# Preparing the next attention group inside the last head of the group ahead of it

## The chip, the cores and the metric

The kernel runs on one core of a Trainium2 chip. The metric is the device time of one execution in microseconds (us). The core has five engines with queues of their own: TensorE (PE in the rows, its weight loads PEld), VectorE (DVE), ScalarE (ACT), GpSimd (POOL) and SyncE (SP); POOL and SP also issue the DMAs.

## What is computed

Two transformer blocks on 512 tokens of width 1024, in float32. The second block runs two mixers on the same input, an RWKV-7 recurrence and a sparse attention (NSA) of 16 heads in 4 groups that share keys and values, merges them by gates, and goes on with a cross attention and a feed-forward part. The change lies in the sparse attention, which for each head sums three branches, each with a gate of its own:

```python
s_c = einsum(qb, k_cmp) * scale + group_bias(...)        # compressed keys: 31 of them
p_c = masked_softmax(s_c, ...)
o_c = einsum(p_c, v_cmp)
...
p_s = masked_softmax(s_s, (dist_s >= 0)...)              # selected blocks
o_s = einsum(p_s, v_g)
...
p_w = masked_softmax(s_w, m_w...)                        # window
o_w = einsum(p_w, vw_b)
out = gb[..., 0:1] * o_c + gb[..., 1:2] * o_s + gb[..., 2:3] * o_w
```

At 512 tokens the selection takes every block and the window covers the sequence, so branches 1 (selected) and 2 (window) are both causal attention over 512 keys, with different keys and values.

## The kernel before

The matmuls take float32 operands split into a high and a low part. `split` makes such a pair from one tile: ScalarE casts the high part (L162), VectorE subtracts it to get the low one (L163). For scores, `q_stack` (L285 on ScalarE, L286 on VectorE) puts both parts of a head's queries into one tile, and `k_stack` loads a key twice by two DMAs (`k_load`, L292) and splits it.

Tiles come from tagged pools with a fixed number of slots. The program is written as generators; a scheduler then sets the order of the instructions of each engine, with the order in which they are emitted as their priority. A tile's writer waits until the readers of the slot's last tile are done.

The phase "pa2" (L1452 on) weaves three streams by rates: `nsa` (190), the RWKV back part followed by the merge (240), and tiles of the merge gates (65). Each `yield` of a stream says how much it has emitted. RWKV's tiles carry the names psa_b and psb_b, the merge gates' psg_m. The loads of `nsa` go to POOL's queue (`self.side`), as do the merge gates' weights (ws).

`nsa` takes the groups g = 0 to 3 in pairs. A pair loads its values and splits them into the tile vt (L1117 to L1120; one slot). Then each group does its preparation and its four heads:

- preparation: four query stacks from two loads, the key stack of branch 1 from a third load, the key stack of branch 2 by a load that is issued here; a memset of kz on POOL (L1128) and copies of the compressed keys into it (L1130); eight matmuls for the compressed scores (L1134), the bias added (L1135), transposes (L1138), the softmax (L1142 to L1154, with the Exp on ScalarE at L1147), transposes back (L1157), and the split into the pair pc; then a `yield`
- for each head: the bias load (L1169, two slots), the product of pc and the compressed values into the PSUM bank pso (L1174), then for branches 1 and 2 the function `attend`, with a `yield` behind each. `attend` does the scores (L311, L312), the reduction with the bias (L313 on VectorE), the Exp (L315), the scaling (L321, L323), the transposes (L328), the split of the transposed probabilities into pt (L330, L331) and the products with vt (L332, L333). `o_evac` (L340, L341) then moves pso into the tile o, and after every second head o is stored to ynd (L1183) from SP's queue. The merge later reads ynd back (cast at L1202)

At head 2 of a group `nsa_loads` issues the loads for the next group: two of queries (L1051), the bias of the compressed scores (L1053, a tile of tag f) and the key of branch 1. All keys, queries and values share the three slots of the tag ld.

Other lines of the rows: L842 (a ScalarE copy of RWKV's), L834, L852, L858 and L883 (others of its copies), L777 and L778 (its solve on VectorE), L875, L889 and L897 (its state steps), L874 (its matmul), L957 (the evacuation of a merge-gate tile), L222 and L209 (the cast and the load of weights).

Of the kernel before, what the change touches and what calls it, by code (L numbers as in the profile page):

```python
# [38 lines left out]
class Gen:  # L39
# [998 lines left out]
    def nsa(self):  # L1038

        nc, A, V, S = self.nc, self.A, self.nc.vector, self.nc.scalar  # L1040
        self.ahead = self.nsa_loads(0)
        for gp in range(2):
            yield from self.nsa_groups(gp, *self.cmp)
# [67 lines left out]
    def nsa_groups(self, gp, kc, vc):  # L1111
        nc, A, V, S = self.nc, self.A, self.nc.vector, self.nc.scalar
        VT = self.f("vt", F32R, (128, 4 * 4 * 128)).rearrange("p (t k n) -> p t k n", t=4, k=4)
# [7 lines left out]
        for gl in range(2):  # L1121
            g = 2 * gp + gl
            qs, cb, k1 = self.ahead
            qst = {2 * i + par: self.q_stack(qs[i], par, -0.125) for i in range(2) for par in range(2)}
            kst = {1: self.split(k1, tag="kst"), 2: self.k_stack(self.kvd[6 + gp], gl)}

            kz = self.f("kz", F32R, (128, 448)).rearrange("p (i n) -> p i n", i=2)
            nc.gpsimd.memset(kz.bitcast(F32), 0.0)  # L1128
            for i, k in enumerate(kc):
                S.copy(kz[:, i, 96:128], k[:, 32 * g:32 * g + 32].bitcast(F32))  # L1130
            ps = self.ps("a")
            for h in range(4):
                for i in range(2):
                    nc.tensor.matmul(ps, kz[:, i, 96 - 32 * h:224 - 32 * h], qst[h], start=h + i == 0, stop=h + i == 4)  # L1134
            V.tensor_tensor(cb, ps, cb, OP.add)  # L1135
            ps = self.ps("b")
            for i in range(4):
                nc.tensor.transpose(ps[:, i * 128:i * 128 + 128], cb[:, i * 128:i * 128 + 128], self.ident)  # L1138
            v16 = ps.rearrange("p (a n) -> p a n", n=32)
            st = self.f("sm", shape=(128, 32))  # L1140
            m, s_ = st[:, 0:16], st[:, 16:32]
            V.tensor_reduce(m, v16, AX.X, OP.min)  # L1142
            V.tensor_scalar(m, m, 1e29, None, op0=OP.min)
            e = self.f("f")
            ev = e.rearrange("p (a n) -> p a n", n=32)
            V.tensor_tensor(ev, v16, m[:, :, None].to_broadcast([128, 16, 32]), OP.subtract)
            S.activation(e, e, AF.Exp, scale=-1.0)  # L1147
            V.tensor_reduce(s_, ev, AX.X, OP.add)
            V.tensor_scalar(s_, s_, 1e-30, None, op0=OP.max)
            V.reciprocal(s_, s_)  # L1150
            c0 = 12 * g
            V.tensor_tensor(s_.rearrange("p (i h) -> p i h", i=4), s_.rearrange("p (i h) -> p i h", i=4),
                            self.gt[:, :, c0:c0 + 12:3], OP.mult)
            V.tensor_tensor(ev, ev, s_[:, :, None].to_broadcast([128, 16, 32]), OP.mult)  # L1154
            ps = self.ps("b")
            for i in range(4):
                nc.tensor.transpose(ps[:, i * 128:i * 128 + 128], e[:, i * 128:i * 128 + 128], self.ident)  # L1157
            pc = self.split(ps, tag="pc")
            yield 6.0
            O = None  # L1160
            for h in range(4):
                hd = 4 * g + h
                par = h % 2
                if par == 0:
                    O = self.f("o")
                if h == 2 and g < 3:
                    self.ahead = self.nsa_loads(g + 1)
# [438 lines left out]
```

## Time and profile before

| | us |
|---|---|
| median of 3 runs | 2092.48 (2091.06 to 2099.59) |
| profiled execution | 2094.42, its span 2092.6 |
| mean granted TensorE clock | 0.975 of full |
| TensorE busy | 2015.6 (96%) |
| VectorE busy | 1308.9 (63%) |
| ScalarE busy | 926.1 (44%) |

The span is what the trace covers, from 0 to 2092.6 us; all times of rows are counted from its start. Busy shares are means over stages with different limits, so the stretches in the rows below are the view to go by. A row of a timeline gives the start, the duration of a run of like instructions, the engine, the line, the operation with output and inputs, and in brackets how long the engine idled before it and which instruction ended that.

### The profile page before, as it was taken

How to read it: one execution, taken by the hardware profiler on the slowest of the kernel's cores; microseconds unless marked ns; L12 is line 12 of the kernel's file. 1: busy time of each engine (PE TensorE's matmuls, PEld its weight loads, DVE VectorE, ACT ScalarE, POOL GpSimd, SP SyncE). 2: the span in 40 equal slices, each digit the busy share in tenths (PEclk: the TensorE clock that was granted, in tenths of full speed). 3: DMA queues.
4: the chain of work that ended last, by engine and by line, in shares of the span. 5: the costliest groups of instructions: out<-in, count | busy, mean ns of one | idle time of the engine just before them, and what ended most of it. 6: DMA issues, size and time to landing. Idle time of an engine off the chain costs nothing. (4 is left out here: it accounts for less than half of the span.)

```text
span 2092.6 us, 27828 instructions
## 1 busy us (share of the span) xinstructions
PE 2015.6 (96%) x9927; PEld 1635.5 (78%) x9927; DVE 1308.9 (63%) x3007; ACT 926.1 (44%) x1778; POOL 95.4 (5%) x167
## 2 busy tenths in 40 slices
PE   8999999999999999899989899999999999999999
PEld 7778888888887778777767688877878878888887
DVE  5785432554464569777668788878466756666522
ACT  5864531442253233233357477767143443333311
POOL 0000000000003201000120111000000000000000
PEclk9999999999999999999989799999999999999999
DMA  4223333333365655555574454445542123323332
GB/s 161 80 89 95 94 92 100 107 115 117 125 199 159 165 158 164 154 149 175 161 178 109 116 131 129 110 131 160 158 145 81 51 80 91 97 95 92 100 108 83
DMA packets 178266, 256.75 MB, mean 123 GB/s; under 512 B 95408, under 2 KB 109952, under 8 KB 178128
## 3 DMA queue, kind: packets, MB, share of 16 engines
q1 hardware_dynamic: 162832, 231.31, 38.1%
q0 software_dynamic: 15296, 23.66, 4.0%
q8 instruction: 79, 1.29, 0.3%
q14 instruction: 59, 0.48, 0.1%
HBM read 205.12 MB, written 45.53 MB: 120 GB/s over the span
## 5 line engine op out<-in xcount | busy, mean ns | idle before, releaser
L222 ACT CAST wh<-ws 128x1024 fp32r<-128x1024 f32 (+2 forms) x283 | 291.7, 1031 | 699.6 <-PE psg L244 459.4
L223 DVE TENSOR_TENSOR wl<-ws,wh 128x1024 fp32r<-128x1024 f32 (+2 forms) x283 | 339.5, 1201 | 263.5 <-ACT wh L222 262.3
L243 PE MATMUL psg<-xh,wh 128*128 128x512 f32 x984 | 392.1, 399 | 2.9 <-ACT wh L222 2.9
L245 PE MATMUL psg<-xh,wl 128*128 128x512 f32 x984 | 393.6, 400 | 0.0
L244 PE MATMUL psg<-act,wh 128*128 128x512 f32 x912 | 359.7, 395 | 1.1 <-DVE act L166 1.1
L243 PEld LDWEIGHTS psg<-xh,wh 128*128 128x128 f32 x984 | 185.9, 189 | 45.0 <-ACT wh L222 3.7
L245 PEld LDWEIGHTS psg<-xh,wl 128*128 128x128 f32 x984 | 186.1, 189 | 41.6 <-issue 1.2
L244 PEld LDWEIGHTS psg<-act,wh 128*128 128x128 f32 x912 | 171.1, 188 | 42.8 <-DVE act L166 1.5
L243 PE MATMUL psg<-act,wh 128*128 128x512 f32 x496 | 196.2, 397 | 2.8 <-ACT act L165 1.4
L245 PE MATMUL psg<-act,wl 128*128 128x512 f32 x496 | 196.0, 396 | 0.5 <-DVE wl L223 0.5
L244 PE MATMUL psg<-xl,wh 128*128 128x512 f32 x352 | 139.7, 397 | 0.0
L243 PEld LDWEIGHTS psg<-act,wh 128*128 128x128 f32 x496 | 92.8, 187 | 27.3 <-ACT act L165 2.2
L245 PEld LDWEIGHTS psg<-act,wl 128*128 128x128 f32 x496 | 93.0, 187 | 23.8 <-DVE wl L223 1.3
L315 ACT ACTIVATE p<-p,sm 128x128 f32<-128x128 f32 (+3 forms) x160 | 89.6, 561 | 18.8 <-DVE sm L313 17.7
L244 PE MATMUL psg<-x,wh 128*128 128x512 f32 x216 | 88.7, 411 | 0.0
L331 DVE TENSOR_TENSOR pt<-psb,pt 128x512 fp32r<-128x512 f32 (+3 forms) x160 | 75.6, 487 | 18.7 <-ACT pt L330 16.6
L313 DVE CUSTOM_DVE_ANT_0 p<-psa,bias 128x128 f32<-128x128 f32 (+3 forms) x160 | 76.0, 484 | 11.9 <-PE psa L312 9.7
L328 PE MATMUL psb<-ident,p 128*128 128x128 f32 x400 | 79.1, 292 | 2.2 <-DVE p L323 1.2
L330 ACT CAST pt<-psb 128x512 fp32r<-128x512 f32 (+3 forms) x160 | 65.9, 424 | 32.0 <-PE psb L328 29.4
L244 PEld LDWEIGHTS psg<-xl,wh 128*128 128x128 f32 x352 | 66.3, 188 | 14.1
L243 PE MATMUL psg_p<-xh,wh 128*128 128x512 f32 x176 | 72.8, 414 | 0.8 <-ACT f L957 0.6
L244 PE MATMUL psg_p<-x,wh 128*128 128x512 f32 x176 | 72.3, 411 | 0.0
(491 smaller groups left out, 3916.4 us busy)
## 6 DMA issues: line engine op xcount, KB each, us to landing
ws<-in_w_in SPq DMA_DIRECT2D x49, 512.0 KB, 4.0
ws<-in_w_fup SPq DMA_DIRECT2D x44, 512.0 KB, 3.5
ws<-in_w_up SPq DMA_DIRECT2D x32, 512.0 KB, 3.5
ws<-in_w_down SPq DMA_DIRECT2D x32, 512.0 KB, 3.6
ws<-in_w_fdn SPq DMA_DIRECT2D x16, 512.0 KB, 3.6
ws<-in_w_qku SPq DMA_DIRECT2D x12, 512.0 KB, 3.6
ws<-in_w_in POOLq DMA_DIRECT2D x10, 512.0 KB, 4.8
ws<-in_w_out SPq DMA_DIRECT2D x8, 512.0 KB, 3.5
```

The source lines that it names most:

```text
L222: nc.scalar.copy(wh[:, :n], ws[:, :n])
L223: nc.vector.tensor_tensor(wl[:, :n], ws[:, :n], wh[:, :n].bitcast(F32), OP.subtract)
L243: nc.tensor.matmul(p[:, :n], wh[:, s], h[:, :n], start=c + k == 0, stop=False)
L244: nc.tensor.matmul(p[:, :n], wh[:, s], l[:, :n], start=False, stop=False)
L245: nc.tensor.matmul(p[:, :n], wl[:, s], h[:, :n], start=False, stop=last)
L313: nc.vector.tensor_tensor_reduce(pt, ps[:, :w], bias[:, 512 - w:], 1.0, 3e38, OP.add, OP.min, m[:, i:i + 1])
L315: nc.scalar.activation(pt, pt, AF.Exp, bias=m[:, i:i + 1], scale=-1.0, accum_out=s[:, i:i + 1])
L328: nc.tensor.transpose(ps[:, (i - j) * 128:(i - j + 1) * 128], P[i][:, j * 128:j * 128 + 128], self.ident)
L330: nc.scalar.copy(ph[:, :w], ps[:, :w])
L331: nc.vector.tensor_tensor(pl[:, :w], ps[:, :w], ph[:, :w].bitcast(F32), OP.subtract)
```

## The change

`nsa_groups` is cut in three. `nsa_pre(g)` holds the query stacks, the key stack of branch 1, and the whole compressed softmax up to pc, with three yields of 2.0 in place of one of 6.0. `nsa_values(gp)` holds the values. `nsa_group(g, ...)` holds the key stack of branch 2, the values when g is even, and the heads. The preparation of group 0 is emitted at the start; that of group g + 1 is emitted in head 3 of group g, behind branch 1 and ahead of branch 2. The query stacks get five slots for four, the output tile o one for two. The loads for the next group stay at head 2.

```diff
@@ nsa
-        for gp in range(2):
-            yield from self.nsa_groups(gp, *self.cmp)
+        pre = yield from self.nsa_pre(0)
+        for g in range(4):
+            pre = yield from self.nsa_group(g, *pre)
@@ nsa_groups, nsa_pre, nsa_values
-    def nsa_groups(self, gp, kc, vc):
+    def nsa_pre(self, g):
...
+        qs, cb, k1 = self.ahead
+        qst = {2 * i + par: self.q_stack(qs[i], par, -0.125) for i in range(2) for par in range(2)}
+        kst = {1: self.split(k1, tag="kst")}
...
+        V.tensor_tensor(cb, ps, cb, OP.add)
+        yield 2.0
...
+        S.activation(e, e, AF.Exp, scale=-1.0)
+        yield 2.0
...
+        pc = self.split(ps, tag="pc")
+        yield 2.0
+        return qst, kst, pc
+
+    def nsa_values(self, gp):
...
-            kst = {1: self.split(k1, tag="kst"), 2: self.k_stack(self.kvd[6 + gp], gl)}
...
-            yield 6.0
@@ nsa_group
+    def nsa_group(self, g, qst, kst, pc):
...
+        kst[2] = self.k_stack(self.kvd[6 + gp], gl)
+        if gl == 0:
+            self.nsa_values(gp)
+        VT = self.VT
+        for h in range(4):
...
+            ready = self.nsa_pre(g + 1) if h == 3 and g < 3 else iter(())
+            for br in (1, 2):
+                kv = 2 * (br - 1) + gl
+                self.attend(qst[h], kst[br], bias, lambda j: VT[:, j, kv], o,
+                            False, br == 2, gate=self.gt[:, :, 3 * hd + br])
+                yield 3.6
+                if br == 1:
+                    try:
+                        while True:
+                            yield next(ready)
+                    except StopIteration as done:
+                        pre = done.value
+            self.o_evac(O, o, par)
...
@@ emit
-            with g.phase("pa2", f=3, ld=3, qst=4, kst=6, p=2, pt=4, bias=2, pc=2, kz=1, o=2, ot=1, vt=1,
+            with g.phase("pa2", f=3, ld=3, qst=5, kst=6, p=2, pt=4, bias=2, pc=2, kz=1, o=1, ot=1, vt=1,
```

The scheduled order shows where this puts the instructions. The numbers behind names tell tiles apart; they differ between the two programs.

ScalarE at the start of group 0, before (vt is the value tile, vs, wl, et and yi are RWKV's; kst_8959 is the key stack of branch 2):

```order
L162 CAST kst_8952<-ld_8926 128x512
L834 COPY wl_9004<-psa_b_9097 128x512
L1119 CAST vt_8929<-ld_8930 128x8x64
L842 COPY vs_9032<-psa_b_9103 64x4x64
L1119 CAST vt_8929<-ld_8935 128x8x64
L162 CAST kst_8959<-ld_8956 128x512
L1147 ACTIVATE f_8985<-f_8985 128x512
L842 COPY vs_9032<-psa_b_9103 64x4x64
L852 COPY et<-psa_b_9114 32x4x32 x4
```

The same place with the change (kst_9126 is the key stack of branch 2, f_9068 the Exp of the compressed softmax):

```order
L162 CAST kst_8941<-ld_8926 128x512
L834 COPY wl_8961<-psa_b_9054 128x512
L842 COPY vs_8989<-psa_b_9071 64x4x64
L162 CAST kst_9126<-ld_9123 128x512
L842 COPY vs_8989<-psa_b_9071 64x4x64
L1163 CAST vt_9130<-ld_9131 128x8x64
L1163 CAST vt_9130<-ld_9136 128x8x64
L852 COPY et<-psa_b_9082 32x4x32 x3
L1139 ACTIVATE f_9068<-f_9068 128x512
L852 COPY et<-psa_b_9082 32x4x32
```

The first copy into vs (L842) has moved ahead of the value casts, now L1163; the second stands behind the cast of branch 2's key stack, and the value casts and the Exp (now L1139) come last.

VectorE at the start of group 1, before (f_10344 and sm_10341 are the compressed softmax of group 1, bias_10441 is the bias of its head 0):

```order
L1152 TENSOR_TENSOR sm_10341<-sm_10341,gt 128x16
L897 SCALAR_TENSOR_TENSOR vs_9692<-vs_9692,decay,psb_b_10421 64x64
L1154 TENSOR_TENSOR f_10344<-f_10344,sm_10341 128x512
L777 TENSOR_TENSOR ys_9214<-as_9213,ys_9214 128x512
L897 SCALAR_TENSOR_TENSOR vs_9692<-vs_9692,decay,psb_b_10421 64x64
L778 TENSOR_REDUCE ys_9214<-ys_9214 128x16
L163 TENSOR_TENSOR pc_10358<-psb_10352,pc_10357 128x512
L313 ISA p_10447,sm_10446<-psa_10448,bias_10441 128x128
L313 ISA sm_10446 128x1
L313 ISA p_10447,sm_10446<-psa_10453,bias_10441 128x256
```

VectorE at the end of group 0 with the change (bias_9973 is the bias of group 0's head 3, pc_10305 the compressed probabilities of group 1; L154 and L155 are RWKV's norm):

```order
L153 TENSOR_TENSOR sm_10280<-sm_10277 128x8
L313 ISA p_10328,sm_10327<-psa_10334,bias_9973 128x256
L313 ISA sm_10327 128x1
L154 TENSOR_TENSOR sm_10280<-sm_10280,sm_10279 128x8
L313 ISA p_10328,sm_10327<-psa_10339,bias_9973 128x384
L313 ISA sm_10327 128x1
L155 SCALAR_TENSOR_TENSOR sm_10277<-sm_10280,sm_10277 128x8
L163 TENSOR_TENSOR pc_10305<-psb_10299,pc_10304 128x512
L313 ISA p_10328,sm_10327<-psa_10344,bias_9973 128x512
L313 ISA sm_10327 128x1
L777 TENSOR_TENSOR ys_9214<-as_9213,ys_9214 128x450
```

Before, group 1's softmax ended in the split into pc and its own head 0 followed; now that split stands among the score reductions of branch 2 of group 0's head 3, and the reductions of group 1's head 0 follow 19 rows behind this piece. The four reductions of that head's branch 1 stand 63 rows and more ahead.

POOL's queue at the same place, before (ld_10315 is the key load of branch 2 of group 1; ld_9745, ld_9747 and ld_9751 were the prefetch; bias_10441 and bias_10716 are for heads 0 and 1 of group 1):

```order
L292 DMA ld_9751<-kvd 64x512 x2
L1128 MEMSET kz_10322 128x448
L209 DMA ws_10644<-in_w_in 128x1024
L1169 DMA bias_9754<-grd 128x1x512
L1169 DMA bias_9973<-grd 128x1x512
L1169 DMA bias_10441<-grd 128x1x512
L1169 DMA bias_10716<-grd 128x1x512
L292 DMA ld_10315<-kvd 64x512 x2
L1051 DMA ld_10980<-qd 128x512
L1051 DMA ld_10982<-qd 128x512
```

The same queue with the change (ld_10433 is that key load, kz_10156 is for group 1's compressed scores):

```order
L1054 DMA f_9749<-gfd 128x1x512
L1119 MEMSET kz_10156 128x448
L1052 DMA ld_9745<-qd 128x512
L1052 DMA ld_9747<-qd 128x512
L292 DMA ld_9751<-kvd 64x512 x2
L1183 DMA bias_9754<-grd 128x1x512
L1183 DMA bias_9973<-grd 128x1x512
L1183 DMA bias_10441<-grd 128x1x512
L209 DMA ws_10644<-in_w_in 128x1024
L292 DMA ld_10433<-kvd 64x512 x2
```

The key load of branch 2 was queued behind the bias loads of four heads; now those of three stand ahead of it. The memset of kz for group 1 has moved ahead of the prefetch.

ScalarE at the start of group 2, before (vt_11521 is the value tile of the second pair, ot_11517 the output of group 1's head 3):

```order
L1130 CAST kz_12760<-kch 128x32
L340 COPY ot_11517<-pso_11262 64x512
L1119 CAST vt_11521<-ld_11522 128x8x64
L1119 CAST vt_11521<-ld_11527 128x8x64
L915 COPY y_10807<-sm_11406 128x512
L162 CAST kst_11551<-ld_11548 128x512
```

The same place with the change (vt_11701, ot_11690; p_11719 is branch 1 of group 2's head 0, pt_11751 the split of its probabilities):

```order
L315 ACTIVATE p_11821,sm_11820<-p_11821,sm_11820 128x128
L321 ACTIVATE p_11719<-p_11719,sm_11718 128x384
L340 COPY ot_11690<-pso_11262 64x512
L1163 CAST vt_11701<-ld_11702 128x8x64
L1163 CAST vt_11701<-ld_11707 128x8x64
L321 ACTIVATE p_11719<-p_11719,sm_11718 128x512
L883 COPY y_11361<-psa_b_11800 64x64 x2
L315 ACTIVATE p_11821,sm_11820<-p_11821,sm_11820 128x256
L330 CAST pt_11751<-psb_11746 128x512
```

The value casts still follow the evacuation of head 3, the last reader of the value tile; behind them stood the whole preparation, and now stands head 0's own branch 1.

## Rows read from the trace of the kernel before

**Rows 1.** Page, busy time by engine, and granted clock in 40 slices.
```profile
PE 2015.6 (96%) x9927; PEld 1635.5 (78%) x9927; DVE 1308.9 (63%) x3007; ACT 926.1 (44%) x1778; POOL 95.4 (5%) x167
...
PEclk9999999999999999999989799999999999999999
```

**Rows 2.** Stretch, length, busy us of PE PEld DVE ACT POOL; PEclk, DMA share, GB/s.
```profile
1060.00:1070.00 10.00, 5.12 (x23) 3.80 (x21) 5.78 (x14) 3.17 (x6) 3.93 (x7) 0.95 1.00 232
...
1160.00:1170.00 10.00, 6.57 (x33) 4.52 (x33) 9.58 (x24) 2.65 (x7) 2.99 (x6) 1.00 0.47 114
1170.00:1185.00 15.00, 10.95 (x51) 8.80 (x48) 10.93 (x26) 5.31 (x16) 3.03 (x5) 0.66 0.50 152
...
1200.00:1270.00 70.00, 68.66 (x434) 56.80 (x432) 58.76 (x208) 54.39 (x154) 8.19 (x13) 1.00 0.51 128
1270.00:1287.00 17.00, 15.16 (x90) 11.75 (x88) 15.16 (x47) 11.90 (x30) 2.88 (x5) 1.00 0.75 217
...
1297.00:1360.00 63.00, 61.93 (x396) 50.93 (x396) 54.14 (x197) 49.03 (x140) 5.53 (x8) 1.00 0.42 109
1360.00:1380.00 20.00, 19.26 (x105) 16.02 (x105) 13.27 (x39) 11.10 (x32) 0.58 (x1) 0.83 0.61 178
```

**Rows 3.** The same view, of the stretches at the lower clock.
```profile
1068.50:1086.00 17.50, 16.48 (x61) 14.04 (x62) 10.73 (x42) 10.17 (x29) 1.36 (x3) 0.51 0.67 140
1150.60:1157.00 6.40, 5.97 (x24) 5.21 (x25) 5.38 (x18) 3.68 (x9) 0.79 (x1) 0.52 0.14 32
...
1174.60:1198.30 23.70, 20.57 (x78) 17.76 (x78) 15.27 (x54) 10.82 (x32) 2.21 (x3) 0.50 0.38 101
1286.60:1296.80 10.20, 10.13 (x46) 9.40 (x45) 5.03 (x15) 6.55 (x22) 0.00 (x0) 0.54 0.27 66
1372.60:1378.80 6.20, 6.20 (x24) 5.72 (x25) 2.53 (x10) 3.06 (x11) 0.00 (x0) 0.51 0.78 267
```

**Rows 4.** Timeline (start, us, ...), ScalarE and then TensorE at group 0.
```profile
1063.04 0.62 ACT L1119 CAST vt<-ld 128x512 fp32r<-128x512 f32 x1 [5.77 <-DMA ld<-vd]
...
1068.12 0.37 ACT L842 COPY vs<-psa_b 64x256 f32<-64x256 f32 x1 [0.63 <-DVE vs L843]
...
1068.54 0.49 PE L874 MATMUL psb_b<-vs,ws 128*128 128x128 f32 x2 [4.88 <-ACT vs L842]
```

**Rows 5.** Timeline of VectorE and then ScalarE at group 1.
```profile
1161.51 0.69 DVE L286 SCALAR_TENSOR_TENSOR qst<-ld,qst 64x512 fp32r<-64x512 f32 x1
...
1172.07 0.69 DVE L1146 TENSOR_TENSOR f<-psb,sm 128x512 f32<-128x512 f32 x1
...
1175.46 0.69 DVE L1148 TENSOR_REDUCE sm<-f 128x16 f32<-128x512 f32 x1 [1.13 <-ACT f L1147]
...
1182.72 0.69 DVE L163 TENSOR_TENSOR pc<-psb,pc 128x512 fp32r<-128x512 f32 x1 [1.64 <-ACT pc L162]
1183.33 0.28 DVE L313 CUSTOM_DVE_ANT_0 p<-psa,bias 128x128 f32<-128x128 f32 x1
...
1174.28 0.62 ACT L162 CAST kst<-ld 128x512 fp32r<-128x512 f32 x1 [2.03 <-DMA ld<-kvd]
```

**Rows 6.** Timeline of ScalarE and then TensorE at group 2.
```profile
1281.63 0.62 ACT L162 CAST kst<-ld 128x512 fp32r<-128x512 f32 x1 [1.55 <-DMA ld<-kvd]
...
1284.62 0.50 PE L1174 MATMUL pso<-pc,vc 32*128 32x512 f32 x1 [1.10 <-ACT pc L162]
```

**Rows 7.** Groups of instructions, 1040 to 1460: the evacuation and the value subtraction.
```profile
L341 DVE TENSOR_TENSOR o<-pso,ot 64x512 f32<-64x512 f32 x15 | 10.2, 682 | 0.9 <-ACT ot L340 0.7
...
L340 ACT COPY ot<-pso 64x512 f32<-64x512 f32 x15 | 8.7, 579 | 3.7 <-PE pso L333 3.3
...
L1120 DVE TENSOR_TENSOR vt<-ld,vt 128x512 fp32r<-128x512 f32 x4 | 2.7, 688 | 5.0 <-ACT vt L1119 4.9
```

**Rows 8.** Timeline of ScalarE at 1399, and the DMA view: KB, us to landing.
```profile
1399.23 0.62 ACT L1202 CAST qst<-f 128x512 fp32r<-128x512 f32 x1 [3.27 <-DMA f<-ynd]
...
ynd<-o SPq DMA_DIRECT2D x8, 256.0 KB, 2.8
```

More of the change, by code (lines that the diff above doesn't have):

```diff
@@ L1120, in nsa_groups @@
             V.tensor_tensor(v[:, :, :, 64:128], z, v[:, :, :, 0:64].bitcast(F32), OP.subtract)
[L1121 to L1124, printed above, removed]
-            kst = {1: self.split(k1, tag="kst"), 2: self.k_stack(self.kvd[6 + gp], gl)}
[L1127 to L1158, printed above, removed]
-            yield 6.0
[L1160 to L1167, printed above, removed]
-                bias = self.f("bias")
-                self.side.dma_start(bias, bass.AP(tensor=self.grd.tensor, offset=self.grd.offset + hd * 1280 + 127,
-                                                ap=[[576, 2], [-1, 64], [1, 512]]))
-                o = self.ps("o")
-                hs = slice(32 * h, 32 * h + 32)
-                for i in range(2):
-                    nc.tensor.matmul(o, vc[hs, g].rearrange("p s d -> p (s d)"), pc[i][hs], start=i == 0, stop=False)
-                for br in (1, 2):
-                    kv = 2 * (br - 1) + gl
-                    self.attend(qst[h], kst[br], bias, lambda j: VT[:, j, kv], o,
-                                False, br == 2, gate=self.gt[:, :, 3 * hd + br])
-                    yield 3.6
-                self.o_evac(O, o, par)
-                if par == 1:
-                    pr = hd // 2
-                    nc.sync.dma_start(self.ynd[pr], O)
-                    if "y_n" in self.dbg:
-                        nc.sync.dma_start(self.dbg["y_n"][pr * 128:(pr + 1) * 128], O)
@@ new lines, in nsa_group @@
+    def nsa_group(self, g, qst, kst, pc):
+        nc = self.nc
+        gp, gl = g // 2, g % 2
+        vc, pre, O = self.cmp[1], None, None
+        kst[2] = self.k_stack(self.kvd[6 + gp], gl)
+        if gl == 0:
+            self.nsa_values(gp)
+        VT = self.VT
+        for h in range(4):
+            hd = 4 * g + h
+            par = h % 2
+            if par == 0:
+                O = self.f("o")
+            if h == 2 and g < 3:
+                self.ahead = self.nsa_loads(g + 1)
+            bias = self.f("bias")
+            self.side.dma_start(bias, bass.AP(tensor=self.grd.tensor, offset=self.grd.offset + hd * 1280 + 127,
+                                              ap=[[576, 2], [-1, 64], [1, 512]]))
+            o = self.ps("o")
+            hs = slice(32 * h, 32 * h + 32)
+            for i in range(2):
+                nc.tensor.matmul(o, vc[hs, g].rearrange("p s d -> p (s d)"), pc[i][hs], start=i == 0, stop=False)
+            ready = self.nsa_pre(g + 1) if h == 3 and g < 3 else iter(())
[11 more added lines that the diff above has]
+            self.o_evac(O, o, par)
+            if par == 1:
+                pr = hd // 2
+                nc.sync.dma_start(self.ynd[pr], O)
+                if "y_n" in self.dbg:
+                    nc.sync.dma_start(self.dbg["y_n"][pr * 128:(pr + 1) * 128], O)
+        return pre
```

33 lines of the change are left out of this document (31 added, 2 removed).

## The prediction

> **What bounds the kernel now.** I read the page first, then the stretches, then the queues at the four places where a group of heads begins. The page says that TensorE is busy 96% of the span and that its clock is near full except in a few slices [rows 1]. So a change can only gain where TensorE idles, or runs at its lower clock, and the change touches only the phase from about 1040 to 1460 us. The stretches [rows 2] show two kinds there. Inside a group, TensorE is busy 68.66 of 70 us (1200 to 1270) and 61.93 of 63 (1297 to 1360) at full clock; VectorE, at 84 to 86%, is close behind but not the limit. At a group's start it is otherwise: 5.12 of 10 us at 1060, 6.57 of 10 at 1160, 10.95 of 15 at 1170, 15.16 of 17 at 1270, 19.26 of 20 at 1360. At 1160 to 1170 VectorE is busy 9.58 of 10: there it is the bound, with the RWKV solve (lines 777 and 778) and the next group's preparation both on it.
>
> Behind each of these holes the clock falls to half (1.2 of 2.4 GHz) [rows 3]: 17.5 us from 1068.5, 6.4 from 1150.6, 23.7 from 1174.6, 10.2 from 1286.6, 6.2 from 1372.6. At half clock about half of the busy time is lost: 8.1 us at group 0 (16.48 x 0.49), 3.0 + 10.3 at group 1, 4.7 at group 2, 3.0 at group 3. The idle time of the stretches of rows 2 is 4.9 at group 0, 3.4 + 4.1 at group 1, 1.8 at group 2 and 0.7 at group 3. Together that is 44 us, and the change can hardly give back more; the question is how much of it is due to the order.
>
> **The change part by part.** It adds and removes no arithmetic and no bytes: the same matmuls, softmax and loads, in another order. Every term is therefore a wait or a clock stretch that goes, stays or comes.
>
> *Group 0.* There is no head ahead of it, so nothing is hidden. TensorE idles 4.88 us until a copy of line 842 on ScalarE [rows 4]; that copy is queued behind the value casts of line 1119, which waited 5.77 us for their load. The change puts the first copy of line 842 ahead of the value casts, but the second one behind the cast of the second key stack, whose load is now issued ahead of the value loads. The loads land late because the DMA engines are full (share 1.00 from 1060 to 1070 [rows 2]), which the order doesn't cure. Bounds: all of the 4.88 us and half of the 8.1 us of clock go, -9; or the value casts, now last, hold the Exp and the RWKV steps behind them for another landing, +4. I take -1, nearest to the row that stays (the DMA share).
>
> *Group 1.* Today the chain from the first query stack at 1161.51 to the probabilities at 1182.72 takes 21.9 us with its last subtraction, and the first score reduction follows at 1183.33 [rows 5]. The second key stack's cast on ScalarE waited 2.03 us for its load and held the Exp behind it: the Exp's input was complete at 1172.76, its consumer on VectorE came at 1175.46 after idling 1.13. With the change that cast is no part of the preparation, and its load is issued earlier on POOL's queue, so 2 us of the chain go. What does not go is VectorE. In the new order 63 rows of VectorE stand between the last score reduction of head 3's branch 1 and the first one of its branch 2; before, 59 stood between branch 2's last and the next group's first. The preparation is emitted ahead of branch 2, so branch 2 does not run beside it, but behind it: the scarce stretch moves by one branch, and TensorE has there the same RWKV steps and compressed scores as before. Bounds: nothing goes, or 1 us is added by the norm steps that are now inside (0 to +1); or the whole loss of 1160 to 1198 goes, 3.4 + 4.1 idle and 10.3 clock, -18. I take the 2 us of the wait and a fifth of the clock loss, -4, near the lower end, because 9.58 of 10 us on VectorE is the row that stays.
>
> Here a rule speaks against my caution. In rows 3 the clock fell at 1174.6 with TensorE's own waits on ScalarE and VectorE, and came back only at 1198.3, though VectorE was only 64% busy meanwhile. The Trainium skill (TensorE: Matmul & The Clock Gate, "Loop structure matters more than you think") says that a VectorE copy behind matmuls doesn't cost the clock, and a long wait for a DMA does. By it the 2.03 us wait for the load would be the culprit, and with it gone all 10.3 us would return: group 1 would be -12 and the total -18 instead. The trace shows the fall after waits of TensorE that engines, not a DMA, ended, so I don't follow it.
>
> *Group 2.* ScalarE waited 1.55 us for the load of group 3's first keys, ahead of this group's Exps, and TensorE idled 1.10 us until the compressed probabilities were split [rows 6]; then came 10.2 us of half clock. Both waits go: the probabilities are ready before head 0, and merge-gate matmuls stand between the steps. That is -1.1, and of the 4.7 us of clock I take half, -2.4. New is a serial step: the value tile has one slot, so it can be rewritten only after head 3's last product, and head 0's first product now follows that with no preparation between. The path is the evacuation copy of 0.579, the subtraction of 0.682 and the value subtraction of 0.688 [rows 7], some 2 us with nothing else in between, 3 with handovers, against about 2.8 us of other matmuls that stand between the two products on TensorE (15 rows; an estimate from the 0.2 to 0.5 us of their like). So +0.5, and between 0 and +4 if other VectorE work is ahead. Sum -3, bounds -7 to +4.
>
> *Group 3.* 0.7 us of idle and 3.0 of clock [rows 2, 3]. Half of it goes, -2; bounds -3.7 and +2, the latter because the one slot for outputs puts the store of a head pair directly ahead of the loads that read it back for the merge. ScalarE already waits 3.27 us for such a load, and the store takes 2.8 us to land [rows 8]. Elsewhere the one slot costs nothing: it is written again only at the end of the next head, and a head lasts some 22 us (four of them from the hole at 1270 to the one at 1360 [rows 2]), against the 2.8 of the store; without that cover it would cost that 2.8 each time. The query stack's fifth slot is what lets the new stacks be written while head 3 uses its own.
>
> *Sum.* -1 - 4 - 3 - 2 = -10 us on the profiled execution's 2094.42 (span 2092.6). That execution was 1.9 us above the median of the runs shown, 2092.48, so the forecast is **2082.5 us**, a change just within the 0.5% (10.5 us) that a measurement of this kernel can tell from none.
>
> **The rivals.**
>
> *It hides it all.* The preparation is a VectorE and ScalarE regime of small operations, the heads are a TensorE regime; woven, the holes at groups 1 to 3 close and the clock stays up: -18 at group 1, -7 at group 2, -3.7 at group 3, about -29, 2063.5 us. For it: the clock is a lever, since the 4.1 us of idle after 1170 came with a clock loss of 10.3. Against it: rows 2 show VectorE the bound at 1160, and 84% busy even inside a group, so there is little room for it in another head. The Trainium skill (Perfetto Trace Analysis, "Optimization Strategy") holds that where the busiest engine changes over time, interleaving the regimes may help. Rows 2 bear that rule out for groups 2 and 3, where it is TensorE against VectorE, but not for group 1, where both sides want VectorE.
>
> *Nothing happens.* The hole moves from the group's border into head 3 and is as deep there; the waits saved were not on the path. -2 to +3, so 2092 us. For it: the row count on VectorE above.
>
> *Slower.* Branch 2 of head 3 is held at all three borders until the softmax of the next group is through, and TensorE, which today starts groups 2 and 3 with head 0's scores in hand, starves there as at group 1. Then each of the two costs what group 1 costs in clock, 10.3 instead of 4.7 and 3.0 (+5.6, +7.3), and the value tile's serial step 2 to 4 us more: about +16, 2108 us. It decides at this point: whether TensorE, between the last product of branch 1 and the first of branch 2 in head 3 of groups 1 and 2, idles as it did from 1170 to 1185 (4.1 us of 15 [rows 2]). Against it: merge-gate matmuls fill both places in the new order.
>
> **How the numbers follow.** The forecast's mechanism 0.50, spread from -4 to -17; all hidden 0.17; nothing 0.20; slower 0.13. A gain over 0.5% comes from all of the second and half of the first: 0.42. No change that can be told comes from the other half and the third: 0.45. Slower: 0.13. The range leaves out about one in ten at each side: below it the better half of the all-hidden case, from 2064 on; above it the larger part of the slower case, from 2099 on, which still takes in +6 from the upper bounds of single terms.
>
> **What would show it.** Right: ScalarE's waits for the second key load and the prefetch are gone from the group starts; group 1 still has a stretch of about 20 us in which VectorE is over 90% busy and TensorE under 75%, only earlier in the order (head 3's branch 1 ahead of it, branch 2 behind); half-clock stretches at groups 2 and 3 are shorter; group 0 still waits for its value loads at full DMA share. Wrong: a half-clock stretch at group 1 of under 10 us (all hidden), or new ones inside head 3 of groups 1 and 2, or an idle TensorE of over 2 us ahead of head 0's first product in group 2 (slower).

## The result and the profile after

The changed kernel took 2082.19 us in the median (2079.53 to 2085.24), the kernel before 2092.48 (2091.06 to 2099.59), five runs of each: a ratio of 0.995 [0.9934, 0.9966], 10.3 us less, against a forecast of 10. In a second set of twelve runs it took 2085.84 us against 2092.12, a ratio of 0.9974 [0.9961, 0.9987]: a gain of some 6 us, sure of its sign, below the 0.5% that the prediction called a difference.

The page of the changed kernel, engines and granted clock:

```profile
PE 2004.5 (96%) x9927; PEld 1627.0 (78%) x9927; DVE 1308.6 (63%) x3007; ACT 925.3 (44%) x1778; POOL 95.5 (5%) x167
...
PEclk9999999999999999999989899999999999999999
```

Beside [rows 1] no engine has more or less to do. TensorE's busy time is 11.1 us shorter for the same 9927 matmuls, and its mean granted clock is 0.981 for 0.975: busy time times clock is 1966 us after and 1965 before. That is the first thing to read here: TensorE did the same work, and the 11.1 us are clock. The order of instructions on all engines is the same in both programs up to the phase of the sparse attention, so what the change did must lie between some 1040 and 1450 us.

To place it, the phase is cut near the evacuations of heads (L341) into nine stretches: the start of group 0; its second and third head; the border to group 1 (last head of group 0, most of the first of group 1); heads of group 1; the border to group 2; heads; the border to group 3; the first head of group 3; the rest. The work in a stretch isn't quite the same in both kernels: the merge gates' matmuls, which fill TensorE's gaps, are 238 over the phase in either, but fall into other stretches. So a row tells where TensorE lost time, and only the sum what that cost. The windows of the changed kernel (columns as in [rows 2]):

```profile
1041.00:1106.00 65.00, 57.12 (x289) 45.91 (x288) 36.06 (x121) 36.77 (x96) 14.99 (x25) 0.89 0.66 159
1106.00:1147.00 41.00, 36.22 (x206) 30.30 (x205) 34.22 (x126) 26.62 (x80) 2.20 (x3) 0.88 0.41 104
1147.00:1203.00 56.00, 46.45 (x252) 37.61 (x251) 48.98 (x140) 30.50 (x88) 8.28 (x13) 0.88 0.48 128
1203.00:1260.00 57.00, 56.32 (x356) 46.80 (x355) 49.10 (x165) 44.71 (x126) 7.32 (x13) 1.00 0.49 127
1260.00:1297.00 37.00, 35.70 (x225) 29.20 (x224) 31.39 (x116) 27.82 (x82) 3.79 (x6) 1.00 0.53 142
1297.00:1346.00 49.00, 47.58 (x305) 39.00 (x304) 42.34 (x145) 39.78 (x112) 3.86 (x6) 1.00 0.50 133
1346.00:1374.00 28.00, 27.16 (x178) 22.79 (x179) 22.49 (x78) 17.32 (x53) 1.40 (x2) 1.00 0.48 132
1374.00:1398.00 24.00, 23.01 (x150) 19.29 (x148) 20.78 (x83) 19.89 (x55) 0.80 (x1) 1.00 0.39 114
1398.00:1442.00 44.00, 40.51 (x219) 31.52 (x217) 37.03 (x115) 33.73 (x90) 0.79 (x1) 0.96 0.56 174
```

The same windows of the kernel before, at the second stretch and at the three borders:

```profile
1104.00:1145.00 41.00, 38.69 (x247) 31.62 (x247) 36.55 (x139) 32.79 (x95) 1.61 (x2) 1.00 0.44 108
1145.00:1205.00 60.00, 49.75 (x221) 39.78 (x220) 46.20 (x132) 26.55 (x78) 7.39 (x12) 0.74 0.42 115
...
1263.00:1300.00 37.00, 34.57 (x195) 29.53 (x194) 28.30 (x88) 23.53 (x65) 5.24 (x9) 0.86 0.53 143
...
1356.00:1384.00 28.00, 27.26 (x155) 22.66 (x153) 20.86 (x64) 17.16 (x48) 1.40 (x2) 0.88 0.47 130
```

In each row two losses can be read: idle time (length less TensorE's busy time) and clock loss (busy time times one less the granted clock). At the border to group 1 the kernel before lost 60 - 49.75 = 10.2 us idle and 49.75 x 0.26 = 12.9 to the clock, the changed one 9.5 and 5.6. But one profile of each kernel isn't enough, as a second one of both showed (runs `before2` and `again` below). Idle + clock loss, in us:

| stretch | before | before, second profile | changed | changed, second profile | change of the mean |
|---|---|---|---|---|---|
| start of group 0 | 9.4 + 7.5 | 8.8 + 7.6 | 7.9 + 6.3 | 8.6 + 6.1 | -2.2 |
| its second and third head | 2.3 + 0 | 2.3 + 0.4 | 4.8 + 4.3 | 4.7 + 6.2 | +7.5 |
| border to group 1 | 10.2 + 12.9 | 11.2 + 6.3 | 9.5 + 5.6 | 9.1 + 7.3 | -4.5 |
| its heads | 1.0 + 0 | 1.0 + 0 | 0.7 + 0 | 0.7 + 0 | -0.3 |
| border to group 2 | 2.4 + 4.8 | 2.3 + 0 | 1.3 + 0 | 1.3 + 0 | -3.4 |
| its heads | 0.6 + 0 | 0.6 + 0 | 1.4 + 0 | 1.3 + 0 | +0.8 |
| border to group 3 | 0.7 + 3.3 | 0.8 + 0 | 0.8 + 0 | 0.8 + 0 | -1.6 |
| its first head | 2.4 + 0 | 2.2 + 1.5 | 1.0 + 0 | 1.0 + 0 | -2.0 |
| the rest | 4.6 + 4.4 | 4.6 + 4.4 | 3.5 + 1.6 | 3.5 + 1.6 | -3.9 |
| sum (rows are rounded) | 33.7 + 33.0 | 33.8 + 20.2 | 30.9 + 17.8 | 31.0 + 21.2 | -9.9 |

The idle time of a program comes back within about 1 us in every stretch and 0.2 in the sum; the clock loss does not. The 12.8 us between the losses of the two profiles of the kernel before are clock alone (their spans, 2092.6 and 2083.8, differ by 8.8), and of the borders to groups 2 and 3, where the first profile has half-clock stretches [rows 3], the second has none. So the part of the gain that is sure is small: 2.8 us of idle time. The clock part is a matter of how often a hole is followed by half clock.

Nor is the -9.9 a finer measure than the medians. The second profile of the kernel before is of the fastest of its ten runs (2085.6 us). And the mean spans of the two pairs, 2088.2 and 2081.7, differ by only 6.6: the phase began at 1037 and 1039 us before, and at 1041 and 1040 after, which the order of instructions, the same up to there, doesn't explain.

### The profile page after: what moved, and what is told of

The parts are those of the page before. It is cut to its first block, busy times and chain, and to the rows that moved or that the text cites. A ratio compares the mean times of both kernels' runs of the same rounds, so it can differ in the third digit from the quotient of the medians.

```text
span 2080.4 us, 27852 instructions
## 1 busy us (share of the span) xinstructions
PE 2004.5 (96%) x9927; PEld 1627.0 (78%) x9927; DVE 1308.6 (63%) x3007; ACT 925.3 (44%) x1778; POOL 95.5 (5%) x167
## 4 chain that ended last, share of the span: by engine, by line
PE 46%; DVE 6%; ACT 3%; issue 2%; DMA 2%; SPq 0%; POOL 0%; DVEq 0%; ACTq 0%; POOLq 0%
PE psg L243 8%; PE psg L245 8%; PE psg L244 8%; PE psg_b L243 1%; PE psg_b L244 1%; PE psg_b L245 1%; PE psb L328 1%; DVE ys L777 1%; PE psg_p L243 1%; PE psg_p L244 1%; PE psg_p L245 1%; PE pso L332 1%; PE psa L744 1%; DVE ys L778 1%; PE pso L333 1%
## 5 line engine op out<-in xcount | busy, mean ns | idle before, releaser
L330 ACT CAST pt<-psb 128x512 fp32r<-128x512 f32 (+3 forms) x160 | 65.8, 424 | 25.7 <-PE psb L328 20.8
```

The source lines that it names most:

```text
L330: nc.scalar.copy(ph[:, :w], ps[:, :w])
```

## Experiments

Two theories stood against each other. One: the overlap gains, because the compressed softmax beside a head leaves fewer waits of TensorE at the borders. The other: the overlap as such gives nothing, and the 10 us are other parts of the edit (slots, the places of the key stack and of the values) or chance. Medians are of 6 to 12 runs of each kernel; each set has its own 27 or 29 runs of the kernel before (medians 2092.12, 2092.49, 2093.3), and the ratios are to those.

**The changed kernel again.** No edit.

> The changed kernel once more, on the chip of the next three, for the spread between runs and a second profile. All theories: 2079 to 2086 us, ratio to before 0.993 to 0.997. If the 4 us that its first profile lost before 1040 us were chance, the second profile does not show them in the same place; if group 1's shorter half-clock stretch (about 10 us for 24) was chance, it is again near 20 here.

Measured: 2085.84 us, 0.9974 [0.9961, 0.9987]. The gain is there and smaller than at first. Its profile gave the fifth column of the table. The half-clock stretch at group 1 comes back with the same length, 10.2 us in both profiles of the changed kernel:

```profile
1167.20:1177.40 10.20, 8.29 (x34) 7.11 (x33) 7.27 (x34) 1.91 (x7) 0.00 (x0) 0.50 0.26 62
...
1167.20:1177.40 10.20, 8.28 (x34) 7.04 (x34) 7.69 (x36) 2.31 (x8) 0.00 (x0) 0.50 0.26 59
```

**The preparation at each group's own start.** Everything else stays as changed: five query stacks, one output slot, branch 2's key stack and the values behind the softmax.

```diff
-            ready = self.nsa_pre(g + 1) if h == 3 and g < 3 else iter(())
+            ready = iter(())
@@ nsa
-        pre = yield from self.nsa_pre(0)
         for g in range(4):
+            pre = yield from self.nsa_pre(g)
             pre = yield from self.nsa_group(g, *pre)
```

> The changed kernel, but each group's preparation emitted at the group's own start, ahead of branch 2's key stack and of the values; slots as changed. Theory 1 (the gain is the waits: the key load of branch 2 no longer stands inside the preparation): keeps more than half of the gain, 6 to 9 us below before, 2083 to 2087. Rival (the gain is the overlap with head 3): within 3 us of before, 2089 to 2095. Rival 2 (key stack and values behind the softmax now delay head 0): slower than before by 3 to 10.

Measured: 2105.85 us, 1.0073 [1.0045, 1.0101]: 14 us slower than before, and 20.0 slower than the changed kernel of the same set. So the overlap is worth about 20 us with these slots, and the rest of the edit costs about 14; the nearest of the three expectations, the second rival, had 3 to 10. The timelines of ScalarE, TensorE and POOL at the border to group 1 show one cost of it:

```profile
1172.01 0.63 ACT L285 ACTIVATE qst<-ld 64x512 fp32r<-64x512 f32 x1 [4.75 <-DMA ld<-qd]
...
1172.95 0.58 PE L332 MATMUL pso<-pt,vt 128*128 128x256 f32 x1 [4.14 <-ACT pt L330]
...
1166.92 0.55 POOL L1054 DMA_DIRECT2D ld<-qd  x1 [2.17 <-DVE kst L163]
```

The query load was issued only at 1166.92, when VectorE's split of the key had released its slot of the tag ld; ScalarE stood 4.75 us at the cast of those queries, with the split of head 3's probabilities (L330) behind it, for which TensorE idled 4.14 us. These queries are not yet needed: the cast is the ninth of a query stack in the phase, four to a group, so it is group 2's, in front of a product of group 0. The run of the slots alone, below, shows what brought it there.

**The overlap at one border or at two.** The same switch with `g + 1 in (1,)`, and with `g + 1 in (2, 3)`; the other groups prepare at their own start.

> Only group 1 is prepared inside head 3 of the group ahead; groups 2 and 3 at their own start. Theory 1 with VectorE as the bound at group 1: the overlap there is worth 0 to 2 us, so the time is that of the kernel with no overlap, within 2 us. Rival (group 1, with the largest loss, gives most of the gain): 5 us or more below the kernel with no overlap.

> Only groups 2 and 3 are prepared inside head 3 of the group ahead; group 1 at its own start. Theory 1: holds the whole gain of the change that overlap gives, 2081 to 2085. Rival (group 1 gives most): 5 us or more above the changed kernel, 2087 or more.

Measured: 2095.61 us, 1.0022 [1.0008, 1.0036], with group 1 alone; 2096.18, 1.0017 [1.0002, 1.0031], with groups 2 and 3 alone. Against the start of all groups at home, 2105.85, the gains are 10.2 and 9.7 us, and their sum, 19.9, is the 20.0 of all three: the borders add up, as far as the run without overlap is known (its interval is some 6 us to either side). The rival held in both runs: half of the gain is at group 1, where the prediction had the scarce stretch only move.

**The kernel before, once more.** No edit; it asks how far a profile and a median of the same program repeat.

> The kernel before, once more, for a second profile beside the next three. All theories: the ratio's interval holds 1. From the second group's first evacuation on, marks of VectorE lay within 0.3 us in two profiles of the changed kernel; if that holds here too, this profile's phase from 1037 to the last evacuation is again 424 us long, and the difference of 14 between the profiles of before and changed is real while the medians differ by 6 to 10; if the first profile was an unlucky one, it is 415 to 420.

Measured: 2093.56 us (2085.6 to 2098.62), 1.0007 [0.9987, 1.0028], the profiled span 2083.8 against 2092.6 in the first profile. The phase, from its start to the last evacuation, took 413 us for 424 in the first profile (409 and 410 in the changed kernel), so the first was an unlucky one. One place shows the difference. This is TensorE's timeline at the border to group 2, and the window behind it:

```profile
1281.28 0.50 PE L1174 MATMUL pso<-pc,vc 32*128 32x512 f32 x1 [0.51 <-ACT pc L162]
...
1283.00:1294.00 11.00, 10.04 (x70) 8.61 (x69) 8.86 (x30) 8.31 (x30) 1.41 (x2) 1.00 0.36 82
```

It is the matmul that idled 1.10 us in [rows 6], before 10.2 us at a clock of 0.54 [rows 3]. Here it idled 0.51, and the clock stayed at 1.00. The same order of instructions, a few tenths of a microsecond apart, either loses 4.8 us or nothing. A price put on such a stretch from one profile is a price of chance.

**The slots alone**, in the kernel before.

```diff
-            with g.phase("pa2", f=3, ld=3, qst=4, kst=6, p=2, pt=4, bias=2, pc=2, kz=1, o=2, ot=1, vt=1,
+            with g.phase("pa2", f=3, ld=3, qst=5, kst=6, p=2, pt=4, bias=2, pc=2, kz=1, o=1, ot=1, vt=1,
```

> The kernel before with the slots of the change alone (five query stacks, one output tile). Theory 1 (slots only make room): within 3 us of before. Rival (the one output slot holds an evacuation, or the fifth stack lets the next stacks be cast earlier): 4 us or more to one side.

Measured: 2100.96 us, 1.0046 [1.0025, 1.0066]: 8.5 us slower, where the prediction had nothing. Timelines of ScalarE and TensorE at the border to group 2, and two windows:

```profile
1288.32 0.62 ACT L162 CAST kst<-ld 128x512 fp32r<-128x512 f32 x1 [5.17 <-DMA ld<-kvd]
...
1290.25 0.69 PE L311 MATMUL psa<-kst,qst 128*128 128x384 f32 x1 [5.69 <-DVE sm L313]
...
1285.00:1295.00 10.00, 4.75 (x13) 3.32 (x14) 2.97 (x12) 3.46 (x10) 0.00 (x0) 0.64 0.37 61
1295.00:1305.00 10.00, 10.00 (x46) 9.43 (x44) 6.12 (x15) 6.54 (x21) 0.83 (x1) 0.50 0.35 90
```

ScalarE waits 5.17 us for a key load (1.55 in [rows 6]) and holds the Exps of the first head behind it; the releaser named for TensorE, a score reduction on VectorE, is the one that came last by the profile. Half clock follows. This border loses 6.2 + 7.1 us (2.4 + 4.8 and 2.3 + 0 before), the start of group 0 11.4 + 9.8 (9.4 + 7.5 and 8.8 + 7.6).

In the scheduled order one output slot by itself moves no instruction, and in the trace VectorE idles ahead of none of the sixteen evacuations, so the one output slot holds none. What moves the order is the fifth query stack: with a slot free, the next group's stack is written earlier, and loads and casts that share slots change places. The ninth cast of a query stack, the first of group 2, shows it, before and with the slots:

```profile
1200.51 0.63 ACT L285 ACTIVATE qst<-ld 64x512 fp32r<-64x512 f32 x1
...
1174.27 0.63 ACT L285 ACTIVATE qst<-ld 64x512 fp32r<-64x512 f32 x1 [5.26 <-DMA ld<-qd]
```

Before, it came after group 1's preparation; now it stands inside it, on a load that ScalarE waits 5.26 us for. How the moved casts and loads add up to 8.5 us is argued from the order; the two slots were not run apart.

**Branch 2's key stack back inside the preparation**, with the preparation at the group's own start. It leaves, of the edit, the slots and the values behind the softmax.

```diff
-        kst = {1: self.split(k1, tag="kst")}
+        kst = {1: self.split(k1, tag="kst"), 2: self.k_stack(self.kvd[6 + g // 2], g % 2)}
@@ nsa_group
-        kst[2] = self.k_stack(self.kvd[6 + gp], gl)
```

> No overlap, as in the run with all preparations at their group's start, but with branch 2's key stack back inside the preparation; the values stay behind it. That run was 14 us above before. Theory A (the key stack behind the softmax kept its load tile, so the next queries' load came late and ScalarE waited 4.75 us for it): back to within 4 us of before. Theory B (the values behind the softmax cost it, by the serial step to head 0's first product): still 8 us or more above before.

Measured: 2101.08 us, 1.0053 [1.0034, 1.0071], 8.6 us above before and so not within 4 us of it: the key stack's place isn't the main cost. Theory B named this time, but not its cause: it is the time of the slots alone (2100.96), and the values behind the softmax cost nothing on top that can be told. From here to all of the edit without overlap it is another 4.8 us, put down to the place of the key stack; that step is less sure than the others, since the two intervals overlap ([1.0034, 1.0071] and [1.0045, 1.0101]). Without overlap, then: slots +8.5, values +0.1, key stack +4.8; the overlap takes off 20.0.

**The same key stack with the overlap.** The edit above in the changed kernel, in search of a faster one.

> The changed kernel with branch 2's key stack inside the overlapped preparation too. Theory A: its load and cast leave the group's start, and load tiles come free earlier: 2 to 5 us below the changed kernel. Theory 1 (VectorE is the bound where the preparation stands, and a seventh and eighth key tile are not there): within 2 us of the changed kernel, or up to 4 us slower, as the cast waits for branch 1 of head 3 to let go of its keys.

Measured: 2089.94 us, 0.9996 [0.998, 1.0013]: 4 us worse than the changed kernel's 2085.84, theory 1's upper bound (the intervals just overlap). With overlap the key stack belongs behind the preparation, where the change has it; without overlap that place cost 4.8. So what one part costs depends on the others, and the sum above holds only in the order in which the parts were taken.

**The merge-gate weights on another queue.** The second and third head of group 0 lose more after the change, +7.5 us, a place that the prediction didn't price. POOL's timeline in the changed kernel:

```profile
1138.12 0.79 POOL L1183 DMA_DIRECT2D bias<-grd  x1 [29.23 <-DVE sm L313]
1140.84 0.59 POOL L209 DMA_DIRECT2D ws<-in_w_in  x1 [1.93 <-DVE sm L318]
```

and in the kernel before:

```profile
1085.60 0.58 POOL L209 DMA_DIRECT2D ws<-in_w_in  x1 [16.14 <-DVE wl L223]
```

A bias load waited 29.23 us for its slot, which a score reduction on VectorE had to release, and the weights stood behind it in the queue: they went out 55 us later than before. Without weights the merge gates' matmuls, which fill TensorE's gaps, can't run. Windows with the tile psg_m alone (columns PE, PEld, ACT), changed:

```profile
1105.00:1146.00 41.00, 2.04 (x6) 0.97 (x6) 0.00 (x0) 0.88 0.39 101
```

and before:

```profile
1104.00:1145.00 41.00, 5.42 (x15) 2.61 (x15) 0.60 (x1) 1.00 0.44 108
```

Six of them instead of fifteen; the others run in later stretches. The experiment moves these weight loads to ScalarE's queue, in the changed kernel (`wact`) and in the one before (`wact_b`):

```diff
-(self.side if self.sx == "_m" else self.nc.sync).dma_start(ws[:, :n], src)
+(self.nc.scalar if self.sx == "_m" else self.nc.sync).dma_start(ws[:, :n], src)
```

> The changed kernel with the merge gates' weight loads issued from ScalarE's queue in place of POOL's. Theory Q (in the changed kernel the weight load stands behind three bias loads on POOL, which wait for their slots, so no merge-gate matmul fills TensorE at heads 2 and 3 of group 0, a new loss of about 7 us): that loss falls from about 10 to 3 us and the time is 3 to 7 us below the changed kernel, 0.993 to 0.996 of before. Rival (the loss there belongs to VectorE, or ScalarE pays for ten DMA issues of 0.5 us): within 2 us of the changed kernel, or slower by up to 5.

> The control: the kernel before with the same edit. Theory Q: nothing was queued behind the bias loads there, so within 2 us of before (0.999 to 1.001). Rival (ScalarE's queue is the better place for these loads in either kernel): 4 us or more below before.

Measured: 2090.32 us, 0.9989 [0.9973, 1.0005], and 2099.3, 1.0027 [1.001, 1.0044]. Locally the edit did what it was to do; the tile psg_m, and all instructions, in that stretch of `wact`:

```profile
1108.00:1149.00 41.00, 6.10 (x15) 2.75 (x15) 0.60 (x1) 0.96 0.45 112
...
1108.00:1149.00 41.00, 37.38 (x229) 31.00 (x227) 36.74 (x135) 30.81 (x87) 1.61 (x2) 0.96 0.45 112
```

Fifteen matmuls are back, and the stretch loses 3.6 + 1.5 us where it lost 4.8 + 4.3. Yet the whole is no faster, where theory Q had it 3 to 7 us faster: the border to group 1 loses 11.6 + 6.7 and that to group 2 3.0 + 1.7 (9.5 + 5.6 and 1.3 in the changed kernel). The control says the same of the kernel before, which has no late weights: the edit alone costs it about 6 us, which neither theory had (eight issues of 0.34 us on ScalarE in its trace are 2.7 of them at most). That the weight loads are late is shown, and that it costs TensorE its filling there; that it is the price of the change in the whole is not, since the cure has a price of its own.

**The bias loads on SP's queue** instead, in the changed kernel, so that nothing stands behind them on POOL (`self.side.dma_start(bias, ...)` becomes `nc.sync.dma_start(bias, ...)`).

> The changed kernel with the bias loads on SP's queue, the merge gates' weights left on POOL's. Theory Q: merge-gate matmuls are back at heads 2 and 3 of group 0, 2 to 6 us below the changed kernel, if SP's own loads for RWKV are not held by the bias loads' waits. Rival (a bias load that waits for its slot holds RWKV's loads on SP): 5 us or more slower than the changed kernel.

Measured: 2099.78 us, 1.0032 [1.0015, 1.0048], some 6 us slower than before and 13 slower than the changed kernel. Here too the stretch itself is mended, with 3.7 us idle and no clock loss:

```profile
1105.00:1146.00 41.00, 37.30 (x238) 30.53 (x237) 36.31 (x131) 31.28 (x91) 0.56 (x1) 1.00 0.39 106
```

Taking the bias loads out of the weights' way isn't a cure of the whole either; which loads on SP's queue they hold up was not followed.

**The preparation behind branch 2** of the last head, not ahead of it.

```diff
-                if br == 1:
+                if br == 2:
```

> The changed kernel with the next group's preparation emitted behind branch 2 of head 3 in place of ahead of it (still in that head's stream, ahead of its evacuation and of the next group's key stack). Theory 1 of the prediction (what matters is which of branch 2 and the preparation VectorE takes first, and it is the bound at group 1): the same within 3 us, with the scarce stretch of group 1 back behind branch 2. Rival (the gain is that branch 2's products fill TensorE behind the preparation): the gain is lost, 2089 us or more.

Measured: 2107.53 us, 1.0069 [1.0046, 1.0092]. The window at the border to group 1:

```profile
1174.00:1206.00 32.00, 22.65 (x86) 18.64 (x86) 22.48 (x64) 8.77 (x25) 2.67 (x4) 0.52 0.41 106
```

For 32 us TensorE is 71% busy at half clock, and VectorE 70%. TensorE's longest wait there is that of the run without overlap, 4.11 us for 4.14, again behind a cast of group 2's queries:

```profile
1177.30 0.58 PE L332 MATMUL pso<-pt,vt 128*128 128x256 f32 x1 [4.11 <-ACT pt L330]
```

All that the overlap gave is gone, though the same work is emitted only one branch later, and theory 1's "same within 3 us" with it. Behind branch 2 nothing of head 3 is left but its evacuation, so this is nearly the kernel without overlap (2105.85): the gain needs branch 2 behind the preparation.

## Why the prediction was right, and which of its steps were not

**The sum** held: -10 forecast, -10.3 measured, -6.3 in the repeat. So did its main reading, that all there is to gain is idle time and clock loss at the borders. Its parts held unevenly. By the table the four terms came to -2.2, -4.5, -3.4 and -3.6, which is -13.7 for -10; two stretches without a term, +7.5 and -3.9, nearly make up for that. That the total came so near is in part luck.

**Group 1, -4 forecast, -4.5 measured** (1.4 of it idle time, the rest clock), by other working. The waits went as expected; the key stack's cast on ScalarE, which waited 2.03 us [rows 5], waits 0.34 at group 1; the one ahead of group 2's Exps, 1.55 us before [rows 6], waits 0.74:

```profile
1157.42 0.62 ACT L162 CAST kst<-ld 128x512 fp32r<-128x512 f32 x1 [0.34 <-DMA ld<-kvd]
...
1295.57 0.62 ACT L162 CAST kst<-ld 128x512 fp32r<-128x512 f32 x1 [0.74 <-DMA ld<-kvd]
```

The stretch that was to stay also stayed: windows at group 1, the first inside the second, have VectorE 97% and TensorE 71% busy for 16 us.

```profile
1178.00:1194.00 16.00, 11.39 (x63) 8.21 (x62) 15.51 (x43) 10.74 (x32) 3.52 (x5) 1.00 0.55 149
...
1170.00:1200.00 30.00, 23.78 (x122) 19.25 (x122) 27.20 (x90) 17.12 (x49) 4.10 (x6) 0.82 0.50 132
```

The step that fell is "branch 2 does not run beside it, but behind it: the scarce stretch moves by one branch". TensorE's timeline has the preparation's first compressed scores (L1125), three of the four score products of branch 2 (L311), and the preparation's last transposes (L1150):

```profile
1155.85 0.48 PE L1125 MATMUL psa<-qst,kz 128*128 128x512 f32 x1
...
1159.66 0.30 PE L311 MATMUL psa<-kst,qst 128*128 128x128 f32 x1
...
1161.31 0.36 PE L311 MATMUL psa<-kst,qst 128*128 128x256 f32 x1
...
1174.57 0.69 PE L311 MATMUL psa<-kst,qst 128*128 128x384 f32 x1
...
1176.72 0.94 PE L1150 MATMUL psb<-ident,f 128*128 128x128 f32 x4
```

Branch 2 does run beside the preparation, and the overlap at group 1 is worth 10.2 us (`only1`); emitted one branch later it is worth nothing (`behind2`). It came out as -4 because the other parts of the edit, which the prediction priced at nothing, take most of that back: without overlap this border loses 13.4 + 13.8 us (`atstart`), more than either profile of the kernel before. A right number with two errors in it is luck; only the experiments on the parts show them. A smaller slip is in the 21.9 us of the chain: 1161.51 [rows 5] is the second of group 1's query stacks; VectorE finished the first at 1093.67, so the preparation began long before.

**"The query stack's fifth slot ... lets the new stacks be written while head 3 uses its own"** and the one output slot that "costs nothing": the slots alone cost 8.5 us (`slots`). For the output slot a reason was given, and it held; the fifth query slot was put at nothing without one. It changes the order that the scheduler makes, and with it where ScalarE waits for loads.

**Group 2, -3 forecast, -3.4 measured.** The serial step of the value tile was priced at 0.5 us: TensorE's timeline has the last product of group 1's head 3, what ran between, and the first product of head 0:

```profile
1286.77 0.22 PE L333 MATMUL pso<-pt,vt 128*128 128x128 f32 x1
...
1290.91 0.46 PE L874 MATMUL psb_b<-vs,ws 128*128 128x128 f32 x2 [0.52 <-DVE vs L897]
1291.49 0.50 PE L332 MATMUL pso<-pt,vt 128*128 128x512 f32 x1
```

There is 4.7 us between the two, and other matmuls cover all but 0.52. But most of the forecast gain, the 2.4 us of clock, was a stretch that the kernel before itself has only sometimes; the 1.1 us of idle time came as forecast (2.4 and 2.3 before, 1.3 after).

**Group 3 and behind it, -2 forecast.** Border and first head together gave -3.6. The 3.27 us wait for the outputs that are read back [rows 8] is gone:

```profile
1402.99 0.62 ACT L1224 CAST qst<-f 128x512 fp32r<-128x512 f32 x1 [0.32 <-PE psa L312]
```

The rest of the phase gained 3.9, which no term had.

**Group 0, -1 forecast, -2.2 measured.** Here the reading of the queue was good. ScalarE and then TensorE in the changed kernel:

```profile
1066.92 0.62 ACT L162 CAST kst<-ld 128x512 fp32r<-128x512 f32 x1 [2.42 <-DMA ld<-kvd]
...
1067.86 0.54 PE L874 MATMUL psb_b<-vs,ws 128*128 128x128 f32 x2 [2.38 <-ACT vs L842]
```

As foreseen the second copy of L842 now waits behind the cast of the second key stack, for 2.42 us of a late load instead of 5.77 [rows 4]; TensorE idles 2.38 where it idled 4.88.

**The step that was missing** is POOL's queue in group 0: the weights of the merge gates behind a third bias load. The row stood in the scheduled orders ahead of the prediction, and had no price; the stretch loses 7.5 us more, of which some 4 come back with the weights on time (`wact`).

**The rival of the clock rule.** The Trainium skill (TensorE: Matmul & The Clock Gate, "Loop structure matters more than you think") sets a long DMA wait against a copy behind matmuls. By it, as the prediction drew it, group 1 would have given 12 us with the load waits gone. The trace doesn't agree: with those waits down to 0.34 us group 1 still lost 5.6 and 7.3 us to the clock. Ahead of the fall at 1167.2 TensorE had only short idle times, which VectorE and ScalarE ended:

```profile
1164.14 0.49 PE L888 MATMUL psb_b<-rh,yi 128*128 128x128 f32 x2 [0.69 <-DVE rh L875]
...
1165.12 0.46 PE L879 MATMUL psa_b<-wh,vu 128*128 128x128 f32 x2 [0.49 <-DVE vu L889]
...
1166.98 1.73 PE L911 MATMUL psn<-blk,y 128*128 128x2 f32 x8 [0.95 <-ACT y L908]
```

ScalarE's longer wait for another load, 4.07 us up to 1171.00, lies almost wholly behind that fall.

**The rival that hides it all** leaned on another page of the Trainium skill (Perfetto Trace Analysis, "Optimization Strategy"), by which interleaving regimes with different busy engines may help. Here it does, by 20 us against the same kernel without it (`atstart`), and at group 1 too, where the prediction had denied it; what remains against the kernel before is 6 to 10.

**Signs.** "a half-clock stretch at group 1 of under 10 us" was to say that all is hidden. It measured 10.2, hardly more, and it was a bad sign: the kernel before shows it by itself. Its second profile has stretches of 6.8 us there, and its two profiles lost 12.9 and 6.3 us to the clock:

```profile
1176.70:1183.50 6.80, 5.56 (x23) 4.87 (x24) 5.33 (x12) 1.45 (x5) 0.98 (x2) 0.50 0.27 84
1187.00:1193.80 6.80, 5.90 (x26) 5.31 (x25) 5.38 (x30) 4.70 (x11) 0.00 (x0) 0.50 0.35 81
```

Idle time would have been the better one: 10.2 and 11.2 before, 9.5 and 9.1 after. New half-clock stretches did come, but at heads of group 0, where no sign looked.

None of the versions that were run beats the changed kernel. Two slots for the value tile, and two output slots beside five query stacks, were not run; nor was the overlap with four query stacks, where the next group's last stack has to wait for head 3 to let go of its own.

## What to carry to other kernels

Split an edit into its parts before believing the sum: this one is +8.5 of slots, some +4.8 of a moved key stack and -20 of overlap, taken in that order, and reads from outside like a small gain. A slot more isn't free where a scheduler sets the order: look at what is written earlier with it, and at what then waits. When a change reorders a queue, price every load that now stands behind one that waits for a slot, also those of streams that the change isn't about. And take two profiles of each kernel before putting a price on a half-clock stretch; here idle time repeated and the clock behind it did not.

## What was not expected of the hardware

Two executions of one program with idle times equal within 0.2 us in the sum (33.7 and 33.8) lost 33.0 and 20.2 us to the granted clock. At one place 1.10 us of idle time was followed by 10.2 us at 0.54, and 0.51 us by none. In its runs the kernel before spread over some 18 us (2082.69 to 2100.78 in the three sets), which is more than the whole effect; the median of three that stood ahead of the prediction could not have told it.
